# A transformer block in float32: three conditioning vectors by ACT scalings and GpSimd adds in place of products in column groups on TensorE

## The chip, the cores and the metric

The kernel runs on one core of one Trainium2 chip. The metric is the device time of one execution in microseconds (us). The engines of the core are named as in the profile: PE is TensorE, PEld its weight loads, DVE is VectorE, ACT is ScalarE, POOL is GpSimd, SP is the queue that issues nearly all loads. Each engine works through its own instructions in order and waits for others through semaphores.

## The reference

One token sequence `x` (512 tokens of 1024) goes through two layers. Each layer has a mixer (an HGRN2 recurrence in the first layer, dilated attention in the second) and a SwiGLU block, all in float32, and each layer's norms, shifts and gates come from a conditioning vector `c`:

```python
cond = jax.nn.silu(c)
for layer in range(DEPTH):
    mod = (cond @ ada_w[layer] + ada_b[layer])[:, None, :]
    sh1, sc1, g1, sh2, sc2, g2 = jnp.split(mod, 6, axis=-1)
    u = rms_norm(h, norm_g[layer, 0]) * (1.0 + sc1) + sh1
    ...                                   # mixer: y from u
    h = h + (1.0 + g1) * rms_norm(y, norm_g[layer, 1])
    u = rms_norm(h, norm_g[layer, 2]) * (1.0 + sc2) + sh2
    y = swiglu_ffn(u, ffn_w_in[layer], ffn_w_out[layer])
    h = h + (1.0 + g2) * rms_norm(y, norm_g[layer, 3])
```

The change is about three of the twelve vectors, `g1`, `sc2` and `sh2` of the first layer: each is a row of 1024 numbers, `cond` (1024 long) times a 1024x1024 block of `ada_w[0]`.

## The kernel before

**Weights as a stream.** All weights come through one list of items (`items`), in order, into two buffers of 128x2048 float32 (`raw`, 1 MB each). A load is issued by SP (L65, for bias rows L59) when the buffer it goes to has been read to the end, and SP issues in the order of the list, so that a load that has to wait holds those behind it. A weight tile ("w" item) is split by ACT into a rounded part `hi` (L83) and by DVE into the rest `lo` (L84), of which three pairs can stand ready; PE multiplies it as three products, `uh*hi`, `ul*hi`, `uh*lo` (L408, L409, L410, called a triple below), eight triples for a block of 128 columns, two blocks a tile.

**The stage of the change.** While the first mixer runs over the twelve tiles of `hgrn_w_in` (w0 to w11 below), the loads of the three vectors are woven between them: chunk A0 behind w1, A1 behind w2, and so on to A11. A vector has two halves of 512 columns (`hf`), a half two chunks (`kq`), and a chunk four slices of 128 rows by 512 columns, one for each of its four pieces of `cond`. A0 and A1 are the first half of vector 2 (`g1`), A2 and A3 its second, A4 to A7 vector 4 (`sc2`), A8 to A11 vector 3 (`sh2`). For vector 2 the bias and norm rows are loaded as items of their own (R0 ahead of A3, R1 ahead of A5).

**What happens with a chunk.** `ada_groups` multiplies each slice on PE with 32 equal columns of `cond / 32` (L222): four matmuls write to four groups of 32 partitions of one PSUM bank, and the second chunk adds to the first. ACT copies the bank to `shared` (L226). `col_fin` (L271) or `row_fin` (L289) then sums over the 128 partitions by a product with ones. The other vectors of the kernel do the sum on DVE (L242, L244) and POOL (L246), and so are left as they are.

**The mixer around it.** Each of eight heads (h0 to h7) has ACT make T, K and Q from PSUM (L1467, L1468, L1475) and scale them (L1345, L1346); DVE makes running products and a reciprocal (L1350, L1356) and several products (L1357 to L1359, L1382, L1383); POOL makes two more products, `k` (L1381) and `q` (L1384). PE does the head's small matmuls (L1392 to L1405, L1412, L1426, L1428); then the output is normed: ACT squares it (L1432), DVE adds (L422), POOL takes the power -0.5 into `orr` (L423), DVE multiplies (L1435) and PE transposes (L1442). Of these small steps a list of due times (`Fillers`) says between which blocks they are written; a scheduler, which plays the program through with its own costs, sets the order on each engine.

Of the kernel before, what the change touches and what calls it, by code (L numbers as in the profile page):

```python
# [12 lines left out]
AF = mybir.ActivationFunctionType  # L13
# [137 lines left out]
def block_kernel(tc, x, c, positions, ada_w, ada_b, norm_g, hgrn_w_in, lower, hgrn_norm_g, hgrn_w_out,  # L151
                 attn_w_in, attn_w_out, ffn_w_in, ffn_w_out, inv_freq, out):
    nc = tc.nc
    act, dve, pool, pe = nc.scalar, nc.vector, nc.gpsimd, nc.tensor
    x2, out2 = x[0], out[0]
    V4 = lambda t: t.rearrange("p (a b) -> p a b", a=4)

    with ExitStack() as ctx:
# [16 lines left out]
        cond_tiles = tcx.enter_context(tc.tile_pool(name="tiled", bufs=1, side="right")).tile([P, KT, 32], F32, name="cond_tiles")  # L175
# [20 lines left out]
        cond = base.tile([P, 8], F32, name="cond")  # L196
# [5 lines left out]
        accs = {}  # L202
# [4 lines left out]
        def acc_place():  # L207
            turns_of_acc[0] += 1
            return shared[:, 2 + turns_of_acc[0] % 2]

        by_pe = lambda l, v: l == 0 and v in (2, 3, 4)

        def ada_groups(l, v, hf, kq):


            def run(raw):
                if kq == 0:
                    accs[l, v, hf] = bank("mm")
                ps, r = accs[l, v, hf], V4(raw)
                for k in range(4):  # L220
                    j = slice(32 * k, 32 * k + 32)
                    pe.matmul(ps[j], cond_tiles[:, kq * 4 + k], r[:, k], start=kq == 0, stop=kq == 1,  # L222
                              tile_position=(0, 32 * k))
                if kq == 1:
                    accs[l, v, hf] = acc_place()
                    act.copy(accs[l, v, hf], ps)  # L226
            return run

        def ada_chunk(l, v, hf, kq):
            if by_pe(l, v):  # L230
                return ada_groups(l, v, hf, kq)

            def run(raw):
                if kq == 0:
                    accs[l, v, hf] = acc_place()
                a = accs[l, v, hf]
                r = V4(raw)
                for k in range(4):
                    kt = kq * 4 + k
                    sc = cond[:, kt:kt + 1]  # L240
                    if kt == 0:
                        dve.tensor_scalar(a, r[:, k], sc, None, op0=OP.mult)  # L242
                    else:
                        dve.scalar_tensor_tensor(a, r[:, k], sc, a, op0=OP.mult, op1=OP.add)  # L244
                if kq == 1:
                    pool.partition_all_reduce(a, a, P, bass.bass_isa.ReduceOp.add)  # L246
            return run

        def ada_item(l, v, hf, kq):
            src = ada_w[l, kq * 512:(kq + 1) * 512, v * D + hf * 512:v * D + (hf + 1) * 512]  # L250
            return ("ada", src.rearrange("(k p) n -> p k n", p=P), ada_chunk(l, v, hf, kq))

        def to_col(dst, rows, k):

            jk = fresh(base, [P, P], "diag", 1)
            dve.tensor_tensor_reduce(jk, rows[:, k * P:(k + 1) * P], ident, 1.0, 0.0, OP.mult, OP.add, dst)

        def col_done(l, v, sl, src=None):
            dst = cols[:, l * 4 + v - (1 if v > 2 else 0), sl]
            dve.tensor_add(dst, dst if src is None else src, abc(l, v)[:, sl])  # L260
            if v in (1, 4):
                dve.scalar_tensor_tensor(dst, dst, 1.0, ngc(l, 0 if v == 1 else 2)[:, sl], op0=OP.add, op1=OP.mult)

        def col_fin(l, v, hf):

            def run(_=None):
                a = accs.pop((l, v, hf))
                if by_pe(l, v):
                    b = bank("b")
                    for k in range(4):  # L270
                        pe.matmul(b[:, k:k + 1], a[:, k * P:(k + 1) * P], ones[:, 0:1], start=True, stop=True)  # L271
                    col_done(l, v, slice(hf * 4, hf * 4 + 4), b[:, 0:4])
                    return
                for k in range(4):
                    c = l * 4 + v - (1 if v > 2 else 0)
                    to_col(cols[:, c, hf * 4 + k:hf * 4 + k + 1], a, k)
                col_done(l, v, slice(hf * 4, hf * 4 + 4))
            return run

        def row_fin(l, v, hf):  # L280

            def run(raw):
                if hf == 0:
                    gates[l, v] = fresh(base, [P, D], "gate", 1)
                g = gates[l, v][:, hf * 512:(hf + 1) * 512]
                a = accs.pop((l, v, hf))
                if by_pe(l, v):
                    b = bank("b")
                    pe.matmul(b, ones, a, start=True, stop=True)  # L289
                    a = b  # L290
                dve.tensor_add(g, a, raw[:, 0:512])
                dve.scalar_tensor_tensor(g, g, 1.0, raw[:, 512:D], op0=OP.add, op1=OP.mult)
            return run
# [118 lines left out]
        def block(whi, wlo, c0, width, ps=None, tok=slice(0, S), kts=range(KT)):  # L412

            ps = bank("mm") if ps is None else ps
            for kt in kts:
                a = kt * width + c0
                three(ps[:, tok], whi[:, a:a + P], wlo[:, a:a + P], uh[:, kt, tok], ul[:, kt, tok], kt == 0, kt == KT - 1)
            return ps
# [1041 lines left out]
        for p in range(4):  # L1460
            tiles = []
            whi, wlo = st.take()
            for k in range(2):
                ps = block(whi, wlo, k * P, 256)
# [7 lines left out]
            for k in range(2):  # L1472
                ps = block(whi, wlo, k * P, 256)
# [223 lines left out]
        for kind, g, i in order[1:]:  # L1697
# [16 lines left out]
            for k in range(2):  # L1714
                ps = block(whi, wlo, k * D, P)
# [40 lines left out]
```

## Time and profile before

| what | us |
|---|---|
| median of 3 runs | 1523.06 (1522.5 to 1523.16) |
| the profiled execution, whole | 1522.93 |
| its span, from first to last instruction | 1521.0 |
| PE busy in the span | 1506.4 |
| first L222 of A0 / of A11 starts | 74.90 / 231.73 |
| w0's first product / w11's | 75.90 / 247.47 |

The profile is of one execution. A row of the timeline reads: start, duration, engine, line of the program, operation, tiles written and read, form, count, and in brackets how long the engine was idle before it and who ended that. A row of a view by line reads: shortest, median and longest duration in ns, first and last start. In a row of a view of groups the busy total and the mean in ns stand behind the bar. An engine's waits count for the time only if PE waits in turn, since PE is busy nearly throughout. An f32 matmul leaves two records.

### The profile page before, as it was taken

How to read it: one execution, taken by the hardware profiler on the slowest of the kernel's cores; microseconds unless marked ns; L12 is line 12 of the kernel's file. 1: busy time of each engine (PE TensorE's matmuls, PEld its weight loads, DVE VectorE, ACT ScalarE, POOL GpSimd, SP SyncE). 2: the span in 40 equal slices, each digit the busy share in tenths (PEclk: the TensorE clock that was granted, in tenths of full speed). 3: DMA queues.
4: the chain of work that ended last, by engine and by line, in shares of the span. 5: the costliest groups of instructions: out<-in, count | busy, mean ns of one | idle time of the engine just before them, and what ended most of it. 6: DMA issues, size and time to landing. Idle time of an engine off the chain costs nothing.

```text
span 1521.0 us, 22710 instructions
## 1 busy us (share of the span) xinstructions
PE 1506.4 (99%) x8943; PEld 1325.7 (87%) x8943; DVE 1024.8 (67%) x1750; ACT 689.5 (45%) x1099; POOL 234.9 (15%) x208
## 2 busy tenths in 40 slices
PE   8999999999999999999999999999999999999998
PEld 6777888898999988889888888988888899999886
DVE  4587867487888897472567686335656978888633
ACT  4443433353444432362456664245645544544231
POOL 1011211031222212040010111000002212221100
PEclk9999999999999999999999999999999999999999
DMA  9654445125333366414544433433212333334521
GB/s 308 185 160 147 150 133 166 56 89 161 112 111 112 111 201 223 137 56 138 167 117 131 120 110 108 150 100 90 78 32 80 100 96 112 109 105 148 199 106 56
DMA packets 205498, 192.79 MB, mean 127 GB/s; under 512 B 6680, under 2 KB 164560, under 8 KB 205392
## 3 DMA queue, kind: packets, MB, share of 16 engines
q1 hardware_dynamic: 203856, 190.87, 40.9%
q8 instruction: 70, 1.15, 0.3%
q0 software_dynamic: 1024, 0.13, 0.2%
q10 hardware_dynamic: 512, 0.35, 0.1%
q14 instruction: 36, 0.29, 0.1%
HBM read 189.17 MB, written 2.16 MB: 126 GB/s over the span
## 4 chain that ended last, share of the span: by engine, by line
PE 93%; issue 2%; ACT 2%; POOL 1%; DVE 1%; DMA 1%; POOLq 0%; DVEq 0%; ACTq 0%
PE ps_mm L408 21%; PE ps_mm L410 20%; PE ps_mm L409 20%; PE ps_b L408 3%; PE ps_b L410 3%; PE ps_b L409 3%; PE ps_a L408 3%; PE ps_a L409 3%; PE ps_a L410 3%; PE ps_mm L1162 1%; ACT junk L444 1%; PE ps_a L1162 1%; PE ps_a L1607 1%; PE ps_a L1589 1%; PE ps_mm L222 1%
## 5 line engine op out<-in xcount | busy, mean ns | idle before, releaser
L408 PE MATMUL ps_mm<-uh,hi 128*128 128x512 f32 (+1 forms) x784 | 297.1, 379 | 0.0
L409 PE MATMUL ps_mm<-ul,hi 128*128 128x512 f32 (+1 forms) x784 | 294.9, 376 | 1.0 <-DVE ul L508 1.0
L410 PE MATMUL ps_mm<-uh,lo 128*128 128x512 f32 (+1 forms) x784 | 295.9, 377 | 0.0
L84 DVE TENSOR_TENSOR lo<-raw,hi 128x2048 fp32r<-128x2048 f32 x76 | 180.4, 2374 | 163.7 <-ACT hi L83 163.6
L83 ACT CAST hi<-raw 128x2048 fp32r<-128x2048 f32 x76 | 145.1, 1909 | 161.1 <-DMA raw<-in_ffn_w_out_dram 45.8
L408 PEld LDWEIGHTS ps_mm<-uh,hi 128*128 128x128 f32 x784 | 147.7, 188 | 34.2 <-issue 8.4
L409 PEld LDWEIGHTS ps_mm<-ul,hi 128*128 128x128 f32 x784 | 147.7, 188 | 26.4 <-DVE ul L508 1.4
L410 PEld LDWEIGHTS ps_mm<-uh,lo 128*128 128x128 f32 x784 | 147.6, 188 | 25.9
L788 ACT CAST hiq<-raw 128x1024 fp32r<-128x1024 f32 x68 | 68.3, 1050 | 65.7 <-DVE raw L776 64.7
L408 PE MATMUL ps_mm<-hi,oh 128*128 128x512 f32 x240 | 94.0, 392 | 0.0
L409 PE MATMUL ps_mm<-lo,oh 128*128 128x512 f32 x240 | 93.4, 389 | 0.0
L246 POOL PARTITION_ALL_REDUCE shared<-shared x14 | 46.4, 3312 | 281.3 <-DVE shared L244 281.2
L244 DVE SCALAR_TENSOR_TENSOR shared<-raw,cond,shared 128x512 f32<-128x512 f32 x98 | 73.2, 747 | 21.4 <-DMA raw<-in_ada_w_dram 19.9
L792 DVE TENSOR_TENSOR loq<-raw,hiq 128x1024 fp32r<-128x1024 f32 x68 | 80.0, 1217 | 0.4 <-ACT hiq L788 0.4
L410 PE MATMUL ps_mm<-hi,ul 128*128 128x512 f32 x192 | 75.9, 395 | 0.0
L409 PE MATMUL ps_mm<-lo,uh 128*128 128x512 f32 x192 | 75.9, 395 | 0.0
L408 PE MATMUL ps_mm<-hi,uh 128*128 128x512 f32 x192 | 74.5, 396 | 0.0
L772 POOL TENSOR_TENSOR raw<-raw 128x512 f32<-128x512 f32 x34 | 54.6, 1605 | 104.2 <-DVE loq L768 47.7
L410 PE MATMUL ps_mm<-hi,ol 128*128 128x512 f32 x176 | 68.5, 389 | 0.0
L776 DVE TENSOR_TENSOR raw<-raw 128x1024 f32<-128x1024 f32 x34 | 41.7, 1225 | 39.1 <-POOL raw L772 39.1
L408 PE MATMUL ps_a<-hi,oh 128*128 128x512 f32 x152 | 59.6, 392 | 0.0
L409 PE MATMUL ps_a<-lo,oh 128*128 128x512 f32 x152 | 59.2, 389 | 0.0
(402 smaller groups left out, 3813.3 us busy)
## 6 DMA issues: line engine op xcount, KB each, us to landing
raw<-in_ada_w_dram SPq DMA_DIRECT2D x40, 1024.0 KB, 5.2
raw<-in_ffn_w_in_dram SPq DMA_DIRECT2D x136, 256.0 KB, 4.3
raw<-in_attn_w_in_dram SPq DMA_DIRECT2D x48, 512.0 KB, 5.2
raw<-in_ffn_w_out_dram SPq DMA_DIRECT2D x22, 1024.0 KB, 4.9
raw<-in_hgrn_w_in_dram SPq DMA_DIRECT2D x12, 1024.0 KB, 5.5
raw<-in_attn_w_in_dram SPq DMA_DIRECT2D x12, 1024.0 KB, 5.1
raw<-in_ffn_w_in_dram SPq DMA_DIRECT2D x10, 1024.0 KB, 5.4
first<-in_ada_w_dram SPq DMA_DIRECT2D x14, 512.0 KB, 7.5
```

The costliest lines, as they stand in the source:

```text
L83: self.nc.scalar.copy(hi, t)
L84: self.nc.vector.tensor_sub(lo, t, hi.bitcast(F32))
L244: dve.scalar_tensor_tensor(a, r[:, k], sc, a, op0=OP.mult, op1=OP.add)
L246: pool.partition_all_reduce(a, a, P, bass.bass_isa.ReduceOp.add)
L408: pe.matmul(ps, ah, bh, start=start, stop=False)
L409: pe.matmul(ps, ah, bl, start=False, stop=False)
L410: pe.matmul(ps, al, bh, start=False, stop=stop)
L772: pool.tensor_add(r[:, 2], r[:, 2], r[:, 0])
L776: dve.tensor_tensor(r[:, 0:2], r[:, 0:3:2], r[:, 1:2].broadcast_to((P, 2, 512)), op=OP.add)
L788: act.copy(hi, src)
L792: dve.tensor_sub(lo, src, hi.bitcast(F32))
L1162: pe.matmul(vbanks[hf, t], a, w, start=e == 0 and which == 0, stop=e == KT - 1 and which == 2)
```

## The change

For the three vectors ACT multiplies each slice of the loaded chunk by its piece of `cond`, in place, and POOL adds the slices up: the first two to the last two (1024 columns), then the two that are left into `shared` (first chunk) or onto it (second chunk). The sum over partitions by ones stays; `col_fin` and `row_fin` change only in the name `in_parts`.

```diff
-        by_pe = lambda l, v: l == 0 and v in (2, 3, 4)
-        def ada_groups(l, v, hf, kq):
+        in_parts = lambda l, v: l == 0 and v in (2, 3, 4)
+        def ada_scaled(l, v, hf, kq):
             def run(raw):
+                r = V4(raw)
+                for k in range(4):
+                    kt = kq * 4 + k
+                    act.activation(r[:, k], r[:, k], AF.Copy, scale=cond[:, kt:kt + 1])
+                pool.tensor_add(raw[:, 0:1024], raw[:, 0:1024], raw[:, 1024:2048])
                 if kq == 0:
-                    accs[l, v, hf] = bank("mm")
-                ps, r = accs[l, v, hf], V4(raw)
-                for k in range(4):
-                    j = slice(32 * k, 32 * k + 32)
-                    pe.matmul(ps[j], cond_tiles[:, kq * 4 + k], r[:, k], start=kq == 0, stop=kq == 1,
-                              tile_position=(0, 32 * k))
-                if kq == 1:
                     accs[l, v, hf] = acc_place()
-                    act.copy(accs[l, v, hf], ps)
+                    pool.tensor_add(accs[l, v, hf], r[:, 0], r[:, 1])
+                else:
+                    a = accs[l, v, hf]
+                    for k in range(2):
+                        pool.tensor_add(a, a, r[:, k])
             return run
```

In the changed program lines from 227 on stand one further down than in the profile of before (L84 and L83 stay, L408 is L409). Its new lines are L219 (scaling), L220 (add of 1024), L223 and L227 (adds of 512). The scheduler gives a new order between w0 and the end of the mixer's heads; SP's order and all that comes behind is as before. Three places:

PE at the start of the stage, where w0's first block follows the products of the step before (`late`). Before:

```order
L1162 MATMUL ps_b_608<-late_518,ul 128x512
L1162 MATMUL ps_b_608<-late_519,uh 128x512
L222 MATMUL ps_mm_707<-raw_621,cond_tiles 32x512 x4
L408 MATMUL ps_mm_720<-uh,hi_615 128x512
L409 MATMUL ps_mm_720<-ul,hi_615 128x512
```

And now:

```order
L1163 MATMUL ps_b_608<-late_518,ul 128x512
L1163 MATMUL ps_b_608<-late_519,uh 128x512
L409 MATMUL ps_mm_721<-uh,hi_615 128x512
L410 MATMUL ps_mm_721<-ul,hi_615 128x512
L411 MATMUL ps_mm_721<-uh,lo_616 128x512
```

The group of A0 (`raw_621`) is gone, as are the other eleven. Up to the transposes L1442 of h0 there were five groups and 78 triples on PE; now there are none and 77.

ACT from the split of w5 (`raw_1022`) to that of w6 (`raw_1035`) and the squares of h0 behind it. Before:

```order
L83 CAST hi_1031<-raw_1022 128x2048
L1475 ACTIVATE Q_1062<-ps_mm_1037 128x512
L1414 COPY state_1069<-ps_b_1065 128x128
L1406 COPY k_958<-ps_a_1092 128x384
L83 CAST hi_1197<-raw_1035 128x2048
L1475 ACTIVATE Q_1122<-ps_mm_1097 128x512
L1432 ACTIVATE aT_1133,oss_1134<-ps_b_1125 128x128 x4
L1414 COPY state_1148<-ps_b_1144 128x128
```

And now, where `raw_900` is A3, `raw_1026` w5, `raw_1035` A4 and `raw_1041` w6:

```order
L219 ACTIVATE raw_900<-raw_900,cond 128x512 x4
L1476 ACTIVATE Q_1068<-ps_mm_1043 128x512
L1415 COPY state_1075<-ps_b_1071 128x128
L1407 COPY k_962<-ps_a_1098 128x384
L83 CAST hi_1037<-raw_1026 128x2048
L1476 ACTIVATE Q_1128<-ps_mm_1103 128x512
L219 ACTIVATE raw_1035<-raw_1035,cond 128x512 x4
L1433 ACTIVATE aT_1139,oss_1140<-ps_b_1131 128x128 x4
L1415 COPY state_1154<-ps_b_1150 128x128
L83 CAST hi_1204<-raw_1041 128x2048
```

The scalings of A3 and A4 have come in; those of A4 stand right ahead of the squares of h0 (L1432, now L1433), and the split of w6 has gone behind them.

POOL from h2's product `k` to the second power. Before:

```order
L1381 TENSOR_TENSOR k_1183<-T_923,fsuf_1167 128x512
L1384 TENSOR_TENSOR q_1182<-qd_1160,fpre_1166 128x512
L423 TENSOR_TENSOR orr_1139<-rv_1140,expo 128x4
L1381 TENSOR_TENSOR k_1287<-T_989,fsuf_1271 128x512
L1384 TENSOR_TENSOR q_1286<-qd_1264,fpre_1270 128x512
L423 TENSOR_TENSOR orr_1251<-rv_1252,expo 128x4
```

And now:

```order
L220 TENSOR_TENSOR raw_900<-raw_900 128x1024
L1382 TENSOR_TENSOR k_1189<-T_927,fsuf_1173 128x512
L227 TENSOR_TENSOR shared<-shared,raw_900 128x512 x2
L1385 TENSOR_TENSOR q_1188<-qd_1166,fpre_1172 128x512
L220 TENSOR_TENSOR raw_1035<-raw_1035 128x1024
L1382 TENSOR_TENSOR k_1294<-T_993,fsuf_1278 128x512
L424 TENSOR_TENSOR orr_1145<-rv_1146,expo 128x4
L223 TENSOR_TENSOR shared<-raw_1035 128x512
L1385 TENSOR_TENSOR q_1293<-qd_1271,fpre_1277 128x512
L424 TENSOR_TENSOR orr_1258<-rv_1259,expo 128x4
```

The adds of A3 and A4 have come in between the heads' products, and the power of h0 (`orr_1145`) now stands behind the 1024 wide add of A4.

More of the change, by code (lines that the diff above doesn't have):

```diff
@@ L267, in run @@
                 a = accs.pop((l, v, hf))
-                if by_pe(l, v):
+                if in_parts(l, v):
                     b = bank("b")
@@ L286, in run @@
                 a = accs.pop((l, v, hf))
-                if by_pe(l, v):
+                if in_parts(l, v):
                     b = bank("b")
```

4 lines of the change are left out of this document (2 added, 2 removed).

## The prediction

> **What bounds the kernel now.** I read the page first. Parts 1 and 2 give busy times and the span in 40 slices, the last row of a part being the engine's busy tenths.
>
> ```profile
> span 1521.0 us, 22710 instructions
> PE 1506.4 (99%) x8943; PEld 1325.7 (87%) x8943; DVE 1024.8 (67%) x1750; ACT 689.5 (45%) x1099; POOL 234.9 (15%) x208
> PE   8999999999999999999999999999999999999998
> ```
>
> TensorE (PE) sets the time; work taken off it is worth its length, as long as PE then waits for nothing. The view of busy time by stretches, for the stretch from 74 to 242 us in which the twelve chunks are used, says how much room the other engines have there (columns: PE, weight loads, DVE, ACT, POOL, granted clock, DMA share, GB/s).
>
> ```profile
> 74.00:242.00 168.00, 168.00 (x1005) 132.02 (x1004) 125.04 (x249) 65.09 (x130) 29.29 (x24) 1.00 0.48 154
> ```
>
> PE has no gap at all and a full clock. DVE is at 74%, ACT at 39%, POOL at 17%. So the gain is what the twelve groups take on PE, and the question is what ACT, POOL, DVE and the loads make of the new work.
>
> **What is removed.** The groups are L222. The view by line gives their count, the timeline of PE the weight load of the first group, the second (87.01) with the matmuls around it, and the last; the last row is the copy that followed each vector half.
>
> ```profile
> L222 PE MATMUL ps_mm<-raw,cond_tiles x96: 592/605/617, 74.9 to 232.2; 128*32 128x512 f32 x96
> 74.90 0.16 PEld L222 LDWEIGHTS ps_mm<-raw,cond_tiles 128*32 128x32 f32 x8 [0.35 <-ACT v_tok L1309]
> 86.46 0.39 PE L409 MATMUL ps_mm<-ul,hi 128*128 128x512 f32 x1
> 86.69 0.39 PE L410 MATMUL ps_mm<-uh,lo 128*128 128x512 f32 x1
> 87.01 1.07 PE L222 MATMUL ps_mm<-raw,cond_tiles 128*32 128x512 f32 x8
> 88.00 0.50 PE L408 MATMUL ps_mm<-uh,hi 128*128 128x512 f32 x1
> 231.73 1.07 PE L222 MATMUL ps_mm<-raw,cond_tiles 128*32 128x512 f32 x8
> 232.73 0.50 PE L408 MATMUL ps_mm<-uh,hi 128*128 128x512 f32 x1
> L226 ACT COPY shared<-ps_mm x6: 581/588/625, 90.5 to 232.9; 128x512 f32<-128x512 f32 x6
> ```
>
> 96 records of 605 ns are not 58 us: the four column groups run beside each other, and starts tell the cost. From L222 to the next L408 it is 0.99 us (87.01 to 88.00) and 1.00 us (231.73 to 232.73). Weight matmuls follow each other every 0.23 us (86.46 to 86.69), while the group starts 0.32 us after the one ahead: 0.09 us more, which only the three groups between two weight blocks have. **12 x 1.00 + 3 x 0.09 = 12.3 us** leave PE. If the step onto the next L408 is partly paid by whatever stands ahead, it is less; I put the lower end at 11 us. The six ACT copies L226 (0.59 us each) go too, and one of the four "mm" banks is no longer held from a vector's first chunk to its second; neither is on the path.
>
> **What is added on ACT.** 48 scalings of 128x512 in place. Nearest rows: L1346 does the same form (Copy, a scale per partition, SBUF to SBUF), and six casts L404 stand back to back.
>
> ```profile
> L1346 ACT ACTIVATE K<-K,omlb x8: 719/736/759, 83.4 to 217.1; 128x512 f32<-128x512 f32 x8
> 256.66 3.22 ACT L404 CAST oh<-oT 128x512 fp32r<-128x512 f32 x6
> ```
>
> Back to back one takes between 3.22 / 6 = 0.54 and 0.74 us; I take 0.65, the middle: 2.6 us a chunk, 31 us in all. ACT goes from 65 to about 93 us of the stretch and hides this by itself. What is not hidden is its order: a scaling waits for its chunk's load, and ACT's PSUM copies behind it wait too.
>
> **What is added on POOL.** Per vector half two adds 1024 wide and three 512 wide. No row has 1024; the nearest adds are 512 and 256 wide.
>
> ```profile
> L772 POOL TENSOR_TENSOR raw<-raw x34: 1277/1617/2210, 373.9 to 1377.9; 128x512 f32<-128x512 f32 x34
> L822 POOL TENSOR_TENSOR shared<-shared 128x256 f32<-128x256 f32 x34 | 26.1, 768 | 196.1 <-DVE shared L821 196.1
> ```
>
> Undisturbed a 512 add takes 1.28 us and 256 columns more cost 1.28 - 0.77 = 0.51, so 1024 take 1.28 + 2 x 0.51 = 2.3, at most twice the 1.62 median, 3.2; I take 2.4. First chunks need 2.4 + 1.3 = 3.7 us, second ones 2.4 + 2.6 = 5.0, all together 6 x 8.7 = 52 us: POOL goes from 29 to 81 us. These spans are longer when DVE works, as the first two of three pairs of rows show.
>
> ```profile
> 168.31 2.29 DVE L84 TENSOR_TENSOR lo<-raw,hi 128x2048 fp32r<-128x2048 f32 x1
> 168.31 3.20 POOL L1381 TENSOR_TENSOR k<-T,fsuf 128x512 f32<-128x512 f32 x1 [21.27 <-DVE T L1359]
> 108.56 1.05 POOL L1384 TENSOR_TENSOR q<-qd,fpre 128x512 f32<-128x512 f32 x1
> 108.63 1.00 DVE L1369 COPY fsuf<-ones 128x4 f32<-128x4 f32 x1 [0.94 <-POOL k L1381]
> 129.35 3.34 DVE L1356 RECIPROCAL ki<-bb 128x512 f32<-128x512 f32 x1
> 131.39 1.05 POOL L1384 TENSOR_TENSOR q<-qd,fpre 128x512 f32<-128x512 f32 x1 [8.27 <-PE ps_b L1428]
> ```
>
> POOL's product, 1.05 us at its shortest, took 3.20 and ended 0.91 us after DVE's subtraction; DVE's four-column copy took 1.00 and ended with POOL's product. So such pairs take turns. The reciprocal and a product beside it (131.39) don't: both took what they take alone. I charge each chunk half of an L84, 1.2 us.
>
> **The loop this makes.** Before, a chunk's buffer was free once PE had read it. Now it is free after load, four scalings and POOL's adds, and SP, which issues loads in order, holds the next chunk and the weight tile behind it. Loads and issues of before:
>
> ```profile
> raw<-in_ada_w_dram SPq DMA_DIRECT2D x14, 1024.0 KB, 5.2
> 76.03 0.37 SPq L65 DMA_DIRECT2D raw<-in_ada_w_dram  x1
> 118.03 0.37 SPq L65 DMA_DIRECT2D raw<-in_ada_w_dram  x1
> ```
>
> A turn is 5.2 + 2.6 + 3.7 + 1.2 = 12.7 us for a first chunk and 14.0 for a second, mean 13.4. PE's pace is (231.73 - 74.90) / 11 = 14.3 us a chunk before and 14.3 - 1.0 = 13.2 after. These are nearly equal, so the cover is thin: over eleven turns the loop loses 11 x 0.2 = 2 us on PE.
>
> The weight tiles have cover. Tile w5 is split by 123.14 + 2.29 = 125.4 and its first product starts at 147.85, 22 us later:
>
> ```profile
> 123.14 2.29 DVE L84 TENSOR_TENSOR lo<-raw,hi 128x2048 fp32r<-128x2048 f32 x1 [4.00 <-ACT hi L83]
> 147.85 0.50 PE L408 MATMUL ps_mm<-uh,hi 128*128 128x512 f32 x1
> ```
>
> Each head's output has less. The chain of head h0, the first that stands behind a scaling on ACT:
>
> ```profile
> 130.85 0.39 PE L1428 MATMUL ps_b<-state,q 128*128 128x128 f32 x2
> 133.98 0.27 ACT L1432 ACTIVATE aT<-ps_b 128x128 f32<-128x128 f32 x1
> 137.48 1.02 POOL L423 TENSOR_TENSOR orr<-rv,expo 128x4 f32<-128x4 f32 x1 [5.04 <-DVE rv L422]
> 139.98 0.68 DVE L1435 TENSOR_TENSOR aT<-ps_b,orr 128x512 f32<-128x512 f32 x1
> 142.95 0.60 PE L1442 MATMUL ps_a<-ident,aT 128*128 128x128 f32 x4
> ```
>
> From L1432 to the end of L1435 it is 139.98 + 0.68 - 133.98 = 6.7 us, and L1442 came 2.3 us after that. In the change A4's scalings stand ahead of L1432. When do they end? A0 is there by 74.90 (the first L222 began on a copy of ACT, not on a load), so A1 is issued at 74.9 + 2.6 + 3.7 + 1.2 = 82.4, against 76.03. Then 14.0 + 12.7 + 14.0 for A1 to A3, and some 3 us for ACT's queue and the bias rows that share the buffers: A4 is issued at 126, against 118.03, has landed at 131.3 and is scaled at 133.9. L1435 ends 6.7 later, at 140.6. PE, rid of five groups and with one triple of weight matmuls (0.68) fewer ahead, is at L1442 at 142.95 - 5 x 1.02 - 0.68 = 137.2. It waits **3.4 us**. Once PE has slipped, later places are late by less; I count the loop's 2 us on top: 5.4, rounded to 5.
>
> **The sum.** The profiled execution took 1522.93 us, 1.9 above its span and 0.13 under the median of 1523.06. 1522.93 - 12.3 + 5 = 1515.6, and on the median's footing **1516 us**. The unknown prices give the stall its ends: with scalings of 0.54 and no turns lost to DVE a turn is 11.8 us, under PE's pace, and nothing is lost; with 0.74, adds of 3.2 (0.8 more a turn) and a whole L84 (1.1 more) a turn is 15.7, 2.5 over the pace, 27 us over eleven turns, of which the weight tiles' lead of 22 us hides nothing for the chain above. That end needs all three prices at their worst; two of them half-way, 14.3 a turn, cost 12 us, and I end the range a little beyond that.
>
> **Rivals.** *Full gain.* The loop turns faster than PE, no chain is late: 1523.06 - 12.3 = 1510.8. For it: ACT and POOL stay under 60%. Against: A4's 8 us.
>
> *Loop eats it.* At 14.3 us a turn PE's wait is 11 x 1.1 = 12 us: 1523, no change. For it: the three prices are near this; against: no row shows all of them high at once.
>
> *Slower: DVE is held up by POOL's adds.* DVE is busy 125 us of what would be 168 - 12 = 156, and waits in order besides. Thirty adds total 52 us; if DVE meets each half-way it stands 26 us, 151 of 156, and its 43 us of idle, mostly waits it cannot move, would have to vanish. If some 18 us of this reach PE through L1435 and the L84 behind it: 1523 - 12 + 18 = 1529. It decides from 12.3 us of waits on. Against: eight reciprocals of 3.34 us, 27 us of DVE's work, let POOL run beside them.
> [...]
>
> **How the numbers follow.** Forecast 0.42; full gain 0.24; loop eats it 0.18; slower by DVE 0.16. A measurement of this kernel can tell about 0.2%, 3 us, from no change. So faster 0.42 + 0.24 = 0.66, same 0.18, slower 0.16. The range from 1510 to 1527 takes in the full gain, the forecast and the loop that eats it, and leaves out most of the slower case, with under 0.05 below.
>
> **What would show it.** L222 gone and PE's busy records 96 fewer; 48 scalings near 0.65 us, 12 adds near 2.4 us and 18 near 1.3; A1 issued near 82 and A4 near 126; a wait of PE at the first L1442 for DVE or POOL of about 3 us; DVE's L84 and L1382 longer beside POOL. If PE shows no wait in the stretch, the full gain was right. I am wrong if PE waits above 12 us there, if a weight tile is late, or if the stages after 250 us, where neither work nor order changes, do not simply start earlier.

## The result, and the profile after

The change made the kernel slower: 1535.38 us (median of four runs, 1531.89 to 1537.16) against 1522.83 for the kernel before on the same chip; the ratio is 1.008 with a 95% interval from 1.0061 to 1.0098. The forecast was 1516, and the range ended at 1527. One slow execution of a run below (e6, 3029 us) is left out of its figures.

First the page, the span and the busy times (the profiled execution took 1534.74 us, 2.0 above its span).

```profile
span 1532.7 us, 22596 instructions
PE 1497.3 (98%) x8847; PEld 1327.1 (87%) x8847; DVE 1052.7 (69%) x1750; ACT 715.3 (47%) x1141; POOL 298.8 (19%) x238
```

The 96 products are gone and PE is busy 9.1 us less, but the span is 11.7 us longer. DVE issues the same 1750 instructions and is busy 28 us longer (1024.8 before). The view by stretches says where; its columns are those of the prediction.

```profile
74.00:242.00 168.00, 151.30 (x871) 127.47 (x870) 146.23 (x223) 88.16 (x169) 84.02 (x50) 0.97 0.44 138
250.00:1500.00 1250.00, 1245.10 (x7426) 1121.58 (x7425) 851.47 (x1413) 586.06 (x903) 201.02 (x167) 1.00 0.39 118
```

In the stretch with the chunks PE stood 16.7 us where it had stood nowhere, DVE went from 125 to 146 us with 26 fewer instructions, and the granted clock fell to 0.97. Behind it PE is as busy as it was (1246.1 of these 1250 us before). The waits of PE between 74 and 260 us (total, times, longest), of which there were none before:

```profile
PE ps_b L1427 <- DVE state L1417: 7.9, 1, 7.9
PE ps_b L1413 <- ACT k L1407: 3.5, 1, 3.5
PE ps_a L1406 <- DVE aT L1402: 2.9, 1, 2.9
PE ps_a L1443 <- ACT Q L1451: 1.8, 1, 1.8
PE ps_b L272 <- DVE cols L261: 1.4, 1, 1.4
PE ps_b L1429 <- DVE state L1417: 0.7, 1, 0.7
```

They sum to 18.2 us. The largest lies where the prediction looked, ahead of the first L1443 (149.12), but at another link: PE waited for the state of the next head, h1, whose copy L1415 stands on ACT right behind h0's squares. Rows of SP, ACT, POOL, DVE and PE on the way to it, in order of time:

```profile
109.11 1.44 POOL L1385 TENSOR_TENSOR q<-qd,fpre 128x512 f32<-128x512 f32 x1 [2.48 <-DVE qd L1359]
110.52 4.11 POOL L223 TENSOR_TENSOR shared<-raw 128x512 f32<-128x512 f32 x1
122.91 2.56 ACT L219 ACTIVATE raw<-raw,cond 128x512 f32<-128x512 f32 x4 [10.98 <-DMA raw<-in_ada_w_dram]
133.05 0.37 SPq L65 DMA_DIRECT2D raw<-in_ada_w_dram  x1
138.34 2.56 ACT L219 ACTIVATE raw<-raw,cond 128x512 f32<-128x512 f32 x4 [6.63 <-DMA raw<-in_ada_w_dram]
141.04 2.34 POOL L220 TENSOR_TENSOR raw<-raw 128x1024 f32<-128x1024 f32 x1 [7.00 <-ACT raw L219]
141.25 2.15 DVE L1366 COPY fpre<-ones 128x4 f32<-128x4 f32 x1
141.81 0.27 ACT L1415 COPY state<-ps_b 128x128 f32<-128x128 f32 x1
144.14 1.36 POOL L1382 TENSOR_TENSOR k<-T,fsuf 128x512 f32<-128x512 f32 x1 [0.76 <-DVE T L1360]
144.52 1.01 DVE L423 TENSOR_SCALAR rv<-oss 128x4 f32<-128x4 f32 x1
145.44 0.34 DVE L1417 SCALAR_TENSOR_TENSOR state<-state,ftot,ps_b 128x128 f32<-128x128 f32 x1
146.85 1.19 PE L1427 MATMUL ps_b<-v_tok,aT 128*128 128x128 f32 x4 [7.85 <-DVE state L1417]
```

Two things happen one behind the other. The 512-wide add of A2 stood on POOL behind a head's product `q` that waited for DVE, and then took 4.11 us, 1.3 when alone, beside DVE's L84; the buffer came free late, so A3 and then A4 (issued at 133.05, not 126) came late; ACT stood 6.63 us for A4, and the state copy L1415, which PE needs, could run only behind the scalings, at 141.81. Then A4's own add began, and DVE's four-column copy L1366, 0.17 us when alone, stood 2.15 us and ended with it; L423 stood 1.01 and ended with POOL's next product. L1417 came at 145.44, and the second one, behind whose end (146.71) PE went on, at 146.37. The two held operations lost 2.8 us between them (2.0 beside the add); most of the rest of the 7.85 goes with the late chunk.

The other waits show the same two roads. Ahead of the 2.9 us (up to 121.90) DVE worked without a gap from 101.94 on. In this stretch L1366 stood 1.46 and 1.29 us beside adds, L1374 and L1375 1.02 and 1.03 beside POOL's products for the heads, all of them 0.16 us when alone; L1402 began 2.1 us after its input was there. The 3.5 us end with ACT's copy L1407, and here ACT had stood for a chunk:

```profile
212.33 2.56 ACT L219 ACTIVATE raw<-raw,cond 128x512 f32<-128x512 f32 x4 [6.05 <-DMA raw<-in_ada_w_dram]
214.79 0.46 ACT L1407 COPY k<-ps_a 128x384 f32<-128x384 f32 x1
```

The 1.8 us are alike: ACT stood 8.75 us until 198.32 for a chunk, scaled it, and then made the Q that PE waited for.

Waits are not all. The same view in slices of 3 us around that place:

```profile
144.00:147.00 3.00, 0.15 (x1) 0.18 (x2) 3.00 (x7) 1.40 (x1) 2.75 (x3) 0.52 0.26 92
147.00:150.00 3.00, 3.00 (x15) 3.00 (x16) 2.90 (x5) 0.99 (x2) 0.91 (x1) 0.50 0.12 46
150.00:153.00 3.00, 3.00 (x15) 2.62 (x15) 2.76 (x5) 1.83 (x9) 1.11 (x2) 0.84 0.56 158
```

The granted clock is 0.50 through the second slice and in parts of the two others, from about 144.1 to 150.9 us. The missing share of the clock, times 3 us, summed over the slices from 75 to 270 us, is 6.8 us. I call this the clock's loss below; 18.2 + 6.8 = 25.0 us.

### The profile page after: what moved, and what is told of

Same layout as the page of the kernel before. It is cut to its first block, busy times and chain, and to the rows that moved or that the text cites. A ratio compares the mean times of both kernels' runs of the same rounds, so it can differ in the third digit from the quotient of the medians.

```text
span 1532.7 us, 22596 instructions
## 1 busy us (share of the span) xinstructions
PE 1497.3 (98%) x8847; PEld 1327.1 (87%) x8847; DVE 1052.7 (69%) x1750; ACT 715.3 (47%) x1141; POOL 298.8 (19%) x238
## 3 DMA queue, kind: packets, MB, share of 16 engines
q0 software_dynamic: 1024, 0.13, 0.2%
## 4 chain that ended last, share of the span: by engine, by line
PE 71%; DVE 9%; DMA 7%; ACT 5%; issue 5%; POOL 3%; SPq 0%; POOLq 0%; DVEq 0%; ACTq 0%
PE ps_mm L409 15%; PE ps_mm L411 15%; PE ps_mm L410 15%; PE ps_b L409 3%; PE ps_b L411 3%; PE ps_b L410 3%; PE ps_a L409 3%; PE ps_a L410 3%; PE ps_a L411 3%; DMA raw<-in_ada_w_dram 3%; DVE lo L84 2%; PE ps_mm L1163 1%; DMA raw<-in_ffn_w_in_dram 1%; ACT junk L445 1%; DMA raw<-in_hgrn_w_in_dram 1%
## 5 line engine op out<-in xcount | busy, mean ns | idle before, releaser
L409 PE MATMUL ps_mm<-uh,hi 128*128 128x512 f32 (+1 forms) x784 | 297.9, 380 | 0.0
L410 PE MATMUL ps_mm<-ul,hi 128*128 128x512 f32 (+1 forms) x784 | 296.3, 378 | 1.0 <-DVE ul L509 1.0
L84 DVE TENSOR_TENSOR lo<-raw,hi 128x2048 fp32r<-128x2048 f32 x76 | 182.7, 2404 | 149.8 <-ACT hi L83 149.6
L83 ACT CAST hi<-raw 128x2048 fp32r<-128x2048 f32 x76 | 145.1, 1909 | 137.1 <-DMA raw<-in_ffn_w_out_dram 53.4
L410 PEld LDWEIGHTS ps_mm<-ul,hi 128*128 128x128 f32 x784 | 148.5, 189 | 27.1 <-DVE ul L509 1.4
L409 PEld LDWEIGHTS ps_mm<-uh,hi 128*128 128x128 f32 x784 | 148.5, 189 | 25.7 <-ACT K L1469 0.2
L409 PE MATMUL ps_mm<-hi,oh 128*128 128x512 f32 x240 | 94.1, 393 | 0.0
L410 PE MATMUL ps_mm<-lo,oh 128*128 128x512 f32 x240 | 93.5, 390 | 0.0
L410 PE MATMUL ps_mm<-lo,uh 128*128 128x512 f32 x192 | 76.0, 396 | 0.0
L409 PE MATMUL ps_mm<-hi,uh 128*128 128x512 f32 x192 | 74.6, 396 | 0.0
L823 POOL TENSOR_TENSOR shared<-shared 128x256 f32<-128x256 f32 x34 | 26.1, 767 | 194.9 <-DVE shared L822 194.9
L409 PE MATMUL ps_a<-hi,oh 128*128 128x512 f32 x152 | 59.7, 392 | 0.0
```

What stands on the lines that cost most here:

```text
L83: self.nc.scalar.copy(hi, t)
L84: self.nc.vector.tensor_sub(lo, t, hi.bitcast(F32))
L409: pe.matmul(ps, ah, bh, start=start, stop=False)
L410: pe.matmul(ps, ah, bl, start=False, stop=False)
L823: pool.tensor_add(W[:, 3], W[:, 3], W[:, 5])
```

## The experiments

The table gives each run's time, its ratio to the kernel before (95% interval), what DVE was busy in the whole span (1024.8 before), PE's waits from 74 to 270 us (one sum over the view of waits) and the clock's loss, all in us. Each profile is one execution; that of e16 is the slowest of its eight, 3.5 us above their median.

| run | time | ratio | DVE | waits | clock |
|---|---|---|---|---|---|
| the change | 1535.4 | 1.0080 (1.0061 to 1.0098) | 1052.7 | 18.2 | 6.8 |
| e1 write-only | 1519.1 | 0.9971 (0.9959 to 0.9982) | 1031.8 | 5.6 | 1.7 |
| e2 no scaling | 1528.2 | 1.0032 (1.0021 to 1.0043) | 1053.3 | 13.6 | 3.4 |
| e3 no adds | 1508.2 | 0.9904 (0.9889 to 0.9919) | 1024.3 | 0 | 0 |
| e4 first vector | 1533.4 | 1.0065 (1.0049 to 1.0082) | 1034.1 | 9.7 | 5.1 |
| e5 adds on DVE | 1520.9 | 0.9985 (0.9976 to 0.9995) | 1044.2 | 11.2 | 0 |
| e6 free buffer | 1528.6 | 1.0035 (1.0021 to 1.0050) | 1048.1 | 13.0 | 3.4 |
| e7 last vector | 1525.2 | 1.0010 (1.0000 to 1.0019) | 1029.6 | 2.4 | 3.4 |
| e8 middle vector | 1529.0 | 1.0038 (1.0023 to 1.0053) | 1032.3 | 5.0 | 1.7 |
| e9 short reciprocal | 1532.0 | 1.0060 (1.0045 to 1.0076) | 1029.2 | 15.4 | 5.1 |
| e10 first on DVE | 1524.1 | 1.0007 (0.9998 to 1.0016) | 1033.0 | 4.2 | 1.7 |
| e11 two on DVE | 1520.6 | 0.9985 (0.9976 to 0.9994) | 1037.9 | 4.9 | 1.7 |
| e12 own buffer | 1521.6 | 0.9986 (0.9977 to 0.9996) | 1048.7 | 6.4 | 3.4 |
| e13 own buffer, DVE | 1515.9 | 0.9950 (0.9934 to 0.9967) | 1044.6 | 1.5 | 0 |
| e14 own and free | 1528.3 | 1.0038 (1.0025 to 1.0051) | 1046.5 | 12.6 | 3.4 |
| e15 before, own buffer | 1522.4 | 0.9997 (0.9987 to 1.0006) | 1026.0 | 0 | 0 |
| e16 own later, DVE | 1518.4 | 0.9972 (0.9962 to 0.9982) | 1047.8 | 7.9 | 3.4 |
| e17 own later, GpSimd | 1542.4 | 1.0126 (1.0111 to 1.0142) | 1054.9 | 16.5 | 13.7 |

### Adds, scalings, and what GpSimd reads

e3 takes the adds away and keeps the scalings:

```diff
-                pool.tensor_add(raw[:, 0:1024], raw[:, 0:1024], raw[:, 1024:2048])
-                    pool.tensor_add(accs[l, v, hf], r[:, 0], r[:, 1])
+                    pool.memset(accs[l, v, hf], 0.0)
-                    for k in range(2):
-                        pool.tensor_add(a, a, r[:, k])
```

> The thirty adds are left out; a memset of the sum's place stays for each vector half (0.53 us), so the three vectors are not computed. ACT's 48 scalings stay. Theory A and theory B both expect the gain of 12 us to show: a buffer's turn is 8 us (5.2 + 2.6) and DVE meets nothing, 1510 to 1515. A third theory, C, that the scalings by themselves hold up ACT's PSUM copies (31 us more in ACT's queue, four in a row ahead of a copy): PE waits 6 us or more for ACT and the time is 1518 or more.

It took 1508.2, below what was expected, and its stretch reads like that of before:

```profile
74.00:242.00 168.00, 168.00 (x1026) 142.66 (x1025) 138.14 (x262) 94.73 (x178) 31.98 (x29) 1.00 0.53 170
```

So ACT's scalings by themselves cost nothing (theory C falls), the work taken off PE is worth 15.0 us, not 12.3, and the thirty adds cost 1535.4 - 1508.2 = **27.2 us**. The rest of the study is on where those come from. e1 keeps GpSimd about as long at work (busy 284 us in the whole span, 299 in the change), but lets it only write:

```diff
-                pool.tensor_add(raw[:, 0:1024], raw[:, 0:1024], raw[:, 1024:2048])
+                pool.memset(raw, 0.0)
-                    pool.tensor_add(accs[l, v, hf], r[:, 0], r[:, 1])
+                    (pool.memset(raw[:, 0:1024], 0.0), pool.memset(accs[l, v, hf], 0.0))
-                        pool.tensor_add(a, a, r[:, k])
+                        (pool.memset(raw[:, 0:1024], 0.0), pool.memset(a, 0.0))
```

> GpSimd's thirty adds are replaced by memsets of about the same length that read nothing (raw whole, then half of raw and the sum's place); the sums themselves are left out, so the three vectors are not computed. ACT's scalings, the buffers' turn (load, scalings, some 2 + 1.6 us of GpSimd) and all orders stay nearly as they are. Theory A (turns between GpSimd's two-operand adds and DVE's two-operand work): DVE's busy time from 74 to 240 us falls from 144 back to 124 to 128 us, PE's waits there fall from 18 to under 4 us, and the time is 1511 to 1517. Theory B (the buffers' turn and the scalings at the head of ACT's queue are late, whatever GpSimd reads): the chunks come as late as in the change, A4 issued after 130 us, PE still waits 12 us or more, and the time is 1527 to 1536.

1519.1: 16.3 of the 27.2 us are gone, but not all; it lies between the two theories, nearer to A. A4 was issued at 123.2, 10 us earlier than in the change, so this run takes away most of the lateness together with the holds on DVE and does not tell the two apart. DVE's extra time fell from 28 to 7.5 us (against e3), not to nothing: DVE's small copies end with the memsets too, as these rows of POOL and DVE show.

```profile
112.07 1.11 POOL L227 MEMSET shared<- 128x512 f32 x2
112.07 0.54 DVE L1367 COPY fpre<-dec 128x4 f32<-128x4 f32 x1
112.74 0.46 DVE L1377 COPY f<-dec 128x4 f32<-128x4 f32 x1
```

The two memsets end near 112.6 and at 113.18, the copies, 0.17 us when alone, at 112.61 and 113.20. So my expectation that memsets, which read nothing, leave DVE alone did not hold.

e2 leaves the scalings out and keeps the adds:

```diff
-                for k in range(4):
-                    kt = kq * 4 + k
-                    act.activation(r[:, k], r[:, k], AF.Copy, scale=cond[:, kt:kt + 1])
```

> ACT's 48 scalings are left out; GpSimd adds the unscaled chunks, so the three vectors are wrong. The turn of a buffer is 2.6 us shorter and ACT's queue has nothing in it that waits for a chunk's load. Theory A (turns between GpSimd and DVE): all thirty adds remain, DVE's busy time from 74 to 240 us stays at 140 to 146 us, PE still waits 10 us or more there, and the time is 1525 to 1536. Theory B (late turn, blocked ACT): PE's waits fall under 4 us and the time is 1511 to 1517.

1528.2: as theory A expected, DVE is as full as in the change (1053.3) and PE waits 13.6 us. Still 7.2 us came off, so ACT's queue and the 2.6 us of the turn carry a part.

### One vector at a time

e4, e8 and e7 do the change for one vector (`v in (2,)`, `(4,)` and `(3,)`) and keep the column groups for the others:

```diff
+        scaled = lambda v: v in (2,)
...
-                return ada_scaled(l, v, hf, kq)
+                return (ada_scaled if scaled(v) else ada_groups)(l, v, hf, kq)
```

> Only the first of the three vectors (chunks A0 to A3) is scaled by ACT and added by GpSimd; the other two stay column groups on PE. PE is rid of 4 us: 1519 with no wait. Theory A: DVE pays in proportion to the adds, 20 / 3 = 7 us more busy time, and has room for it at this end of the stretch (PE's first large wait in the change was at 139 us): PE waits under 2 us and the time is 1518 to 1521. Theory B: A3's load and scaling are late (in the change ACT stood 11 us for it until 122 us), so PE waits 3 us or more around 122 to 147 us and the time is 1522 or more.

> Only the middle vector (chunks A4 to A7) is scaled by ACT and added by GpSimd. PE is rid of 5 us. Theory B, one late place made by the first chunks: 1518 to 1520. Theory A, every add its share: 1525 to 1528. With the first and the last vector alone it also tells whether the three losses add up to that of the change (27 us).

> Only the last of the three vectors (chunks A8 to A11) is scaled by ACT and added by GpSimd; the others stay on PE. PE is rid of 4 x 1.2 = 5 us. If the loss is one place that the first chunks make late (theory B with the first vector's 15 us), it is not here: PE waits under 2 us, 1518 to 1520. If every add costs its share (theory A: 27 us over three vectors, 9 us each): 1525 to 1528.

A third of e3's gain is 5.0 us, so each of them would take 1518.0 with no loss. They lost 15.4, 11.0 and 7.2 us: 33.6 together, more than the 27.2 of all three at once (waits and clock in the table show 14.8, 6.7 and 5.8 of these; the rest is not in those columns). The first vector came out as theory B had it, the last in the interval of theory A and the middle one a little above it. The loss isn't one place, and isn't the same for each vector either. The first one alone already costs PE these two waits:

```profile
PE ps_mm L223 <- DMA raw<-in_ada_w_dram: 6.2, 1, 6.2
PE ps_a L1424 <- DVE aT L1420: 3.5, 1, 3.5
```

The former is a chunk that came late (L223 is a column group there), as theory B has it, the latter ends with DVE.

### The same adds on DVE, and DVE's time

e5 gives the adds to DVE, which had to be full then:

```diff
-                pool.tensor_add(raw[:, 0:1024], raw[:, 0:1024], raw[:, 1024:2048])
+                dve.tensor_add(raw[:, 0:1024], raw[:, 0:1024], raw[:, 1024:2048])
```

The 512-wide ones are edited alike.

> The thirty adds are issued by DVE in place of GpSimd; all three vectors are computed, GpSimd has its old work alone. A 1024-wide add should take half an L84 (2.29 / 2 = 1.15 us) and a 512-wide one 0.6 to 0.7, so DVE gets 6 x (2 x 1.15 + 3 x 0.65) = 25 us more, about what it loses to GpSimd's adds in the change (20 us), and a buffer's turn is 9.6 us instead of 11.5 to 12.8 undisturbed. Theory A (DVE's time is what is short; how it is lost does not matter): DVE full, PE waits 8 us or more, 1520 to 1532. Theory B (the late turn of the buffers is what hurts): the chunks come as early as without adds, PE waits under 4 us, 1508 to 1514.

1520.9 and 11.2 us of waits, in the intervals of theory A. But DVE was busy 19.9 us more than in e3 (28.4 in the change) and the time was 14.5 us less than the change's: how DVE's time is lost does matter. e9 asks the other way round. It keeps GpSimd's adds and gives DVE time back:

```diff
-            dve.reciprocal(ki, bb)
+            dve.tensor_copy(ki, bb)
```

> The changed kernel with all scalings and all of GpSimd's adds, but each head's reciprocal (3.35 us on DVE, eight of them in the stretch) is a plain copy of the same size (some 0.3 to 0.7 us), so the first mixer's output is wrong; DVE has 21 to 24 us less to do and GpSimd as much as before. Theory A (DVE's time is what is short): PE's waits from 74 to 260 us fall under 6 us and the time is 1509 to 1518. Theory B (the late turn of the buffers and ACT's queue, with DVE only a bystander): PE still waits 12 us or more, 1526 to 1536.

DVE's busy time in the stretch is back near the 125 us of before the change, and PE still waits 15.4 us:

```profile
74.00:242.00 168.00, 152.55 (x873) 127.69 (x872) 127.30 (x243) 87.60 (x169) 87.29 (x53) 0.97 0.45 144
```

1532.0, only 3.4 us better, and in the interval of theory B. So **how full DVE is does not set the loss**; theory A in that form falls. What stays is at the old place, the state of h1, again in order of time:

```profile
134.05 2.56 ACT L219 ACTIVATE raw<-raw,cond 128x512 f32<-128x512 f32 x4 [6.63 <-DMA raw<-in_ada_w_dram]
136.75 2.35 POOL L220 TENSOR_TENSOR raw<-raw 128x1024 f32<-128x1024 f32 x1 [1.23 <-issue]
136.77 2.35 DVE L1366 COPY fpre<-ones 128x4 f32<-128x4 f32 x1
139.18 0.72 DVE L1417 SCALAR_TENSOR_TENSOR state<-state,ftot,ps_b 128x128 f32<-128x128 f32 x2
140.04 1.20 PE L1427 MATMUL ps_b<-v_tok,aT 128*128 128x128 f32 x4 [4.64 <-DVE state L1417]
```

The scalings that hold up h1's state on ACT end just when the add of the same chunk begins on GpSimd, and this holds the DVE copy ahead of the state's update. So DVE is not the bystander that theory B made of it, but a shorter reciprocal takes neither the late chunk nor the hold away.

e10 and e11 join the edits of e4 and e5: DVE adds up the first vector (`v in (2,)`), or the first two (`v in (2, 4)`), and the others stay on PE.

> The first vector alone is scaled by ACT, and its ten adds are DVE's; the other two vectors stay column groups on PE; all is computed. PE is rid of 15.0 / 3 = 5 us. With all adds on DVE PE's first wait was at 158 us, behind the first vector. Theory A (DVE's time, lost to GpSimd's adds, is the price; here DVE pays only 8 to 10 us of its own, where it has room): no wait of PE above 1 us up to 150 us, 1518 to 1519.5. Theory B (the turn of the first chunks is late whoever adds): PE waits 3 us or more between 117 and 150 us, as with GpSimd's adds, 1521 or more.

> The first and the middle vector (chunks A0 to A7) by ACT's scalings and DVE's adds, the last one on PE. PE is rid of 10 us. The waits that the kernel with all three had on DVE after 200 us (some 6 us) should be gone, those between 158 and 171 us (4.8 us) stay: 1513 + 5 = 1518. If DVE is full already with two vectors (theory A at its strictest): 1520 or more; if the last vector alone was too much: 1513 to 1516.

e10 took 1524.1, 6 us above what the work taken off is worth, and as theory B said: PE waited 4.2 us for A4, in spite of a DVE without GpSimd's adds.

```profile
PE ps_mm L223 <- DMA raw<-in_ada_w_dram: 4.2, 1, 4.2
```

e11 took 1520.6, as the strictest form of theory A had it, and is no better than all three vectors on DVE.

### The turn of the buffers

e6 lets the 1024-wide add write to a place of its own (`s2`), so that the chunk's buffer is free after it:

```diff
-                pool.tensor_add(raw[:, 0:1024], raw[:, 0:1024], raw[:, 1024:2048])
+                s2 = fresh(tpool, [P, 1024], 'halfsum', 1); pool.tensor_add(s2, raw[:, 0:1024], raw[:, 1024:2048])
```

> The 1024-wide add writes its sum to a place of its own, so a chunk's buffer is free after that add and does not wait for the 512-wide adds; everything is computed, and the adds and the turns they take with DVE stay. A turn is shorter by the 1.3 to 4.1 us that the 512-wide adds took in the change and by GpSimd's products between them. Theory A (DVE's lost time): DVE's busy time from 74 to 240 us stays at 140 us or more and the time at 1528 to 1536. Theory B (late turn): A4 is issued before 127 us in place of 133, PE's waits fall under 8 us, and the time is 1512 to 1522.

A4 was issued at 124.8, as theory B had it, but only 6.8 us came off (1528.6, in theory A's interval), and PE still waits 13.0 us. e12 gives the chunks a buffer of their own. The core of it, in the loader:

```diff
-        t = self.pool.tile([P, 2048], F32, name=f"raw{i}", tag="raw", bufs=self.raws)
+        t = (self.own if kind == "part" else self.pool).tile([P, 2048], F32, name=f"{'own' if kind == 'part' else 'raw'}{i}", tag="own" if kind == "part" else "raw", bufs=1 if kind == "part" else self.raws)
```

e13 is e12 with DVE's adds, e14 is e12 with the sum's own place of e6, e15 the kernel before with that buffer.

> The changed kernel, GpSimd's adds and all, but the twelve chunks have a buffer of their own (8 KB per partition in a place that is free during this stage) beside the two that weight tiles and bias rows keep; everything is computed. A chunk's turn is as long as it was, but no weight tile takes a buffer in between, the first chunk is loaded earlier, and no weight tile waits for a chunk's adds. Theory B (the turn of the two shared buffers is what is late): PE waits under 6 us from 74 to 260 us, 1509 to 1517. Theory A' (what DVE loses to GpSimd's adds, some 28 us in all, is late by itself, wherever the chunks stand): DVE's busy time over the whole kernel stays 20 us or more above that without adds (1024 us), PE waits 12 us or more, 1524 or more.

> The buffer of their own for the chunks, and the adds by DVE; everything is computed. Theory B: with a turn near 10 us nothing is late, PE waits under 3 us, 1508 to 1512. Theory A (DVE's time): no better than the same adds with the shared buffers, 1518 to 1522.

> The buffer of their own, and the 1024-wide sum in a place of its own as in the run that frees the buffer sooner; GpSimd adds; everything is computed. If what is left with a buffer of their own is still the turn (load, scalings, adds): 2 us or more below that run and 1508 to 1514. If what is left is DVE's time lost to the adds: the same as that run within 2 us.

> The kernel before, products on PE and no scalings, with the chunks' buffer of their own: a control. PE has no wait in this stage before, so both theories expect no gain: 1521 to 1524. A gain of 3 us or more would mean that the new buffer helps by itself and not through the turn of the changed kernel.

The control is unmoved (1522.4). e12 came to 1521.6, between the theories. Its larger wait has nothing to do with a late chunk, as the rows of DVE, POOL and PE ahead of it show:

```profile
126.48 2.58 POOL L220 TENSOR_TENSOR own<-own 128x1024 f32<-128x1024 f32 x1
126.73 2.88 DVE L1359 TENSOR_TENSOR qd<-bb,Q 128x512 f32<-128x512 f32 x1
129.14 3.02 POOL L227 TENSOR_TENSOR shared<-shared,own 128x512 f32<-128x512 f32 x2
130.96 2.28 DVE L1351 TENSOR_TENSOR_SCAN bb<-T,head 128x512 f32<-128x512 f32 x1
133.16 0.32 DVE L1417 SCALAR_TENSOR_TENSOR state<-state,ftot,ps_b 128x128 f32<-128x128 f32 x1
133.53 0.64 PE L1429 MATMUL ps_b<-state,q 128*128 128x128 f32 x2 [2.85 <-DVE state L1417]
```

L1359 takes 0.68 and the scan 1.22 when alone; beside the adds they took 2.88 and 2.28, 3.3 us more, right ahead of the 2.85 us that PE waited. e14 shortens the turn further and was 6.7 us worse than e12, which neither of its two expectations had. e13 has no add on GpSimd and no wait above 1.3 us from 74 to 270 us, though its DVE is busy 20 us more than without adds:

```profile
74.00:240.00 166.00, 166.00 (x957) 140.20 (x956) 144.50 (x275) 83.58 (x159) 30.05 (x24) 1.00 0.42 140
```

It took 1515.9, between its two expectations and below both kernels (0.9950 of before, 0.9934 to 0.9967). What it has above e3 is mostly at the start: its first weight product came at 79.8 us, in e3 at 74.5, since ACT scales a chunk (51.87 to 54.43) ahead of an L1138 for which PE waits 3.1 us, and the six products behind the wait take 2.7 us (55.19 to 57.91), where six like them take 1.4 later (63.11 to 64.48). In e12, with the same buffer, the scheduler put that L1138 first, and the first weight product came at 76.0. e16 and e17 take the early load away: the buffer lies where the first stage's tiles were, and the two differ in who adds alone.

> The chunks' own buffer and DVE's adds as before, but the buffer lies in the place that the first stage's tiles leave, so the first chunk is loaded and scaled only once that stage is over; everything is computed. With the early buffer PE began this stage at 79.8 us, 5.4 us later than without adds, and waited for nothing in it. Theory B: the start goes back to 75 us, PE waits under 2 us from 74 to 250 us, 1509 to 1512. If the early load was what kept the chunks ahead (the turn is late again without it): PE waits 4 us or more, 1514 or more.

> The same late buffer of their own, with GpSimd's adds as in the change; everything is computed. It differs from the run ahead of it in who adds alone, and from the change in the buffer alone. Theory B: within 3 us of the run with DVE's adds. Theory A' (GpSimd's adds hold DVE operations that PE waits for, buffer or not): DVE operations of 0.2 to 0.7 us that stand 1 to 3 us beside the adds ahead of PE's waits, and 8 us or more above the run with DVE's adds.

The start went back to 74.8 in e16, but small waits came in the stretch instead: 1518.4, the second of its two expectations. e17, the same with GpSimd's adds, is the slowest of all: 1542.4, as theory A' had it, though its longest wait, 3.6 us, ended with a copy on ACT.

### What follows from them together

Four pairs have the same edit but for who adds:

| buffers and vectors | GpSimd | DVE | difference |
|---|---|---|---|
| shared, all three (change, e5) | 1535.4 | 1520.9 | 14.5 |
| shared, first vector (e4, e10) | 1533.4 | 1524.1 | 9.2 |
| own, early (e12, e13) | 1521.6 | 1515.9 | 5.7 |
| own, later (e17, e16) | 1542.4 | 1518.4 | 24.0 |

The sign is the same each time: on GpSimd the adds cost more than on DVE, with any buffers. In three of the pairs this is the larger part of what the GpSimd kernel loses against e3 (e4 against 1518.0); in e12 it is 5.7 of 13.4, and e13 pays 5.3 there at its start.

The sizes are not clean. DVE's adds are shorter (in e5 1.26 us for a 1024-wide one and 0.73 to 0.76 for a 512-wide one, in the change 2.38 and 1.72 to 1.91), so the turn is shorter with them, and the scheduler gave each program an order of its own. Of the instructions other than the chunks' that start by 300 us, at least 329 of 1480 on PE and 98 of 358 on DVE stand in another order in e5 than in the change; the two pairs with a buffer of their own differ about as much. Only e4 and e10 run nearly the same order (22 of 1480 and 29 of 358); they differ by 9.2 us. With the same adds on GpSimd and one buffer of their own e12 and e17 lie 20.8 us apart, so the buffer's place and the order that goes with it do as much as most of the pairs show. 10.1 of these are waits and 10.2 the clock's loss; what makes them is open.

With DVE's adds a buffer of their own gains 5.0 and 2.5 us, with GpSimd's it gains 13.8 (e12) or loses 7.0 (e17). That late chunks are a second cause rests on the rows: PE waited for a chunk itself in e4 and e10, and in the change for ACT operations behind a chunk's scalings (3.5 and 1.8 us, and the larger part of the 7.9). What each cause is worth by itself is not shown, since GpSimd's adds, themselves held by DVE, are also what makes the chunks late.

## Why the prediction was wrong, point by point

- **Work taken off PE.** The mechanism was right, the size a little low: e3 shows 15.0 us, not 12.3 (its interval is 12.3 to 17). I measured a group up to the start of the next L408 and left out that this product is slow as well. The next two rows of before:

```profile
88.34 0.39 PE L409 MATMUL ps_mm<-ul,hi 128*128 128x512 f32 x1
88.57 0.39 PE L410 MATMUL ps_mm<-uh,lo 128*128 128x512 f32 x1
```

  From the L410 at 86.69 to the L409 at 88.34 it is 1.65 us. Without a group two steps of 0.227 lie there, 0.45. This group costs 1.20, 0.11 more than I charged, and 12.3 + 12 x 0.11 = 13.6; the other 1.4 us stay open.
- **Scalings and adds alone.** 2.56 / 4 = 0.64 us a scaling (0.65 predicted), 2.34 to 2.41 for an undisturbed 1024-wide add (2.4), 1.30 for a 512-wide one (1.3): right. A1 was issued at 81.5 (82.4): right.
- **The price of GpSimd and DVE meeting.** This is the step that failed. I charged "half of an L84, 1.2 us" a chunk, put it into the turn of the buffers alone, where PE's pace covered nearly all of it, and let DVE's chains go free. The adds cost 27.2 us on GpSimd and 12.7 on DVE (e5 against e3), where the sum had 5 for all that was added. The groups of the changed kernel show that the 512-wide adds grew most (L223 and L227 against 1.30 alone):

```profile
L220 POOL TENSOR_TENSOR raw<-raw 128x1024 f32<-128x1024 f32 x12 | 28.6, 2381 | 54.6 <-ACT raw L219 46.3 <-ACT state L1415 8.3
L227 POOL TENSOR_TENSOR shared<-shared,raw 128x512 f32<-128x512 f32 x12 | 20.7, 1722 | 0.7
L223 POOL TENSOR_TENSOR shared<-raw 128x512 f32<-128x512 f32 x6 | 11.5, 1911 | 0.2
```

  But the price came through DVE too: an operation of 0.2 to 1.2 us stood for up to a whole add just ahead of one that PE waits for (2.0 us ahead of the largest wait, 2.4 ahead of the one that ended at 121.90).
- **The turn and A4.** I had A4 issued at 126 and scaled at 133.9; it was 133.05 and 140.9. The 7 us come from A2's turn, 19.35 us where 12.7 was charged: its 512-wide add stood 3.9 us behind POOL's wait for DVE and the product `q`, and then took 4.11. The weight tiles were not late, as predicted.
- **The stall.** 3.4 us at the first L1442 and 2 for the loop, 5 in all; 18.2 us of waits and 6.8 of a lower clock came. The clock's part had no term in the sum, and behind the first place, where I had counted 2 us for the loop, PE waited 7.4 us more.
- **The rival that came true.** "Slower: DVE is held up by POOL's adds" had 0.16, the figure of 26 us on DVE (28 measured) and 1529. Its path was another, though: no wait ended with L1435 (now L1436) or L84, and 5.3 us of the waits ended with ACT. I argued against it with the reciprocals, beside one of which a product on POOL took the 1.05 us that it takes alone. e9 shows that this was no argument: with them gone PE waited nearly as long (15.4 us). And the rival's own reason, a DVE with no time left, was wrong too: in e13 DVE is 20 us busier than without adds and PE waits 1.5 us. What counts is where an operation is held, not what DVE's busy time sums to.
- **What would make it wrong.** "PE waits above 12 us there" was the sign that I named, and it came.

## What to carry to other kernels

That GpSimd is idle does not make work for it free: look at which DVE operations stand right ahead of something that PE waits for, and charge each of them up to a whole GpSimd operation (a copy of 0.17 us stood 2.15 us beside an add of 2.34), not a share of the total. To learn what such work costs, leave it out once (27 us here) and give it once to the other engine (14.5 us less), instead of adding up busy times. Where a scheduler sets the order, compare the orders before giving a difference to the edit. A price per instruction on PE was to be read here to the second instruction behind it.

## What the runs showed of the hardware that I had not expected

PE's granted clock fell to one half during or after some waits, for a few microseconds: in the change for 6.8, 3.4 and 3.4 us. In the table the clock's loss comes in steps of 1.7 us, that is pieces of 3.4 us at half clock (1.7, 3.4, 5.1, 6.8, 13.7). The length of a wait does not decide it. The 2.9 us until 121.90 in the change went by at a clock of 1.00 in all three slices from 117 to 126 us; behind the 1.4 us at L272 (until 245.37) the two slices from 246 us on read 0.58 and 0.85. PE's own row in e7 and the slices of 3 us around it (the first column behind the comma is PE's busy time, the last but two the clock):

```profile
240.03 0.63 PE L1461 MATMUL ps_a<-ident,aT 128*128 128x128 f32 x4 [2.00 <-DVE cols L279]
```

```profile
237.00:240.00 3.00, 1.03 (x5) 0.54 (x4) 2.97 (x7) 0.08 (x1) 2.31 (x3) 1.00 0.89 333
240.00:243.00 3.00, 2.97 (x15) 2.81 (x16) 2.93 (x5) 2.22 (x2) 0.18 (x1) 0.63 0.04 14
243.00:246.00 3.00, 3.00 (x9) 2.32 (x8) 3.00 (x3) 0.27 (x1) 0.00 (x0) 0.50 0.52 125
246.00:249.00 3.00, 3.00 (x13) 2.44 (x13) 0.64 (x3) 0.33 (x1) 0.00 (x0) 0.74 0.96 364
```

The same two views of e5:

```profile
158.19 0.52 PE L1406 MATMUL ps_a<-ident,k 128*128 128x128 f32 x3 [2.08 <-ACT oT L1444]
```

```profile
156.00:159.00 3.00, 0.92 (x6) 0.77 (x6) 2.93 (x5) 2.04 (x2) 0.00 (x0) 1.00 0.53 141
159.00:162.00 3.00, 3.00 (x15) 2.46 (x14) 3.00 (x5) 0.21 (x1) 0.00 (x0) 1.00 0.54 211
162.00:165.00 3.00, 2.63 (x13) 2.05 (x11) 3.00 (x7) 3.00 (x6) 0.00 (x0) 1.00 0.16 34
```

2.00 us were followed by the half clock, 2.08 us were not. What does decide it these runs do not show.
